# A changeover in a hybrid encoder layer: the order of sums, first products, forget gate and norm steps

## The chip, the cores and the metric

The kernel runs on one core of a Trainium2 chip. The metric is the device time of one execution in microseconds (us). Five engines share the work: PE (TensorE, matrix products), DVE (VectorE), ACT (ScalarE), POOL (GpSimd) and SP (SyncE, which only starts transfers here). Each engine runs its own instructions in order.

## The reference, cut to what matters

One layer of an encoder on 1024 tokens and 16 meta tokens put before them (L = 1040), width 1024, all in float32, followed by a mixture of experts.

```python
u = rms_norm(h, norm1_g)
p = u @ w_in                      # 1024 x 5384
a, bv, bg, q, k, v, fg, gates = split(p)
ya = pool_mixer(a) @ w_out_a
yb = silu(layer_norm(depthwise_conv(bv * sigmoid(bg)))) @ w_out_b
logf = log_sigmoid(fg + b_forget)                 # forget gate, 8 heads
yc = forgetting_attention(q, k, v, logf) @ w_out_c   # bias: cumsum of logf
g = sigmoid(gates.reshape(B, L, 3, D))
h = h + (g[:,:,0]*ya + g[:,:,1]*yb + g[:,:,2]*yc) @ w_o
h = h + hier_moe(rms_norm(h, norm2_g))            # 4 groups x 4 experts
out = rms_norm(h[:, 16:], final_g)
```

The change lies between the projection to v and the first attention scores: in the projections to q and to the gates (28 column tiles of 128), the forget gate and the convolution's layer norm.

## The kernel before, in words

Every float32 operand of a product is split into a high part (a cast on ACT, L172) and a low part (a subtraction on DVE, L173); a product is three passes, high by high, low by high and high by low. The transposed u lies in four slots: u4[0] and u4[1] hold the high parts of rows k 0 to 3 and 4 to 7, u4[2] and u4[3] the low parts (slot_94 to slot_97 in the rows below).

`run_jobs` runs jobs in the written order: k for four pairs of heads, then v (`v_all`, matmuls L586, evictions L172, L173 and L592, the last writing the forget gate's input `lf`), the job `forget`, and then `seven`. Long DVE work that has no due time stands in a list `pending`, from which `pump` takes some entries between products; `queue_sums` puts the sums of quarters of u there (L533 to L547, each 128 x 2048).

`seven` computes 14 pairs of column tiles (`PAIRS`: two of q, twelve of the gates). For each pair a product of a 2 x 2 block matrix by a 2 x 2 block of u is done with seven products instead of eight. The left operands are raw quarters of the weights and four POOL sums of them that `load` issues behind its DMA (left operands 1, 2 and 4 are raw quarters, 3, 5, 6 and 7 sums). The right operands are quarters of u (products 1, 2, 3), x (product 5, which is copied into u's place by L635 and L636) and the three sums tq[2], tq[3], tq[4] (products 6, 7, 4). A product is 12 matmuls of 128 x 512 (L678), so there are 98 products and 1176 such matmuls. Products of one pair add up in three PSUM banks: 1, 6, 5 and 3 in the first, 2 in the second, 7 and 4 in the third; pairs alternate between banks 0 to 2 and 5 to 7. After products 1, 6 and 5 ACT copies the bank's content of that moment into a buffer (`kept`, L683), and the next product of that bank adds on; after 2, 5 and 4 DVE adds the copy to a bank (`joined`, L687). `out_` scales and splits q and sends it to DRAM through POOL's queue (L697 to L701), or takes the sigmoid of a gate and sends it through SP's queue. The staging buffers are a ring of seven.

The table `order` sets the products' order; `parts` splits the left operand four products ahead. From product 11 on (counted from 0), one entry of the list `norm` is issued ahead of each product: the layer norm of the convolution in eight tiles of 128 tokens (`norm_steps`), each with five entries: `read` (a DMA), parts, `mean`, `root`, `result`. `mean` and `root` begin with two small matmuls by a matrix of ones (L484). `forget` is one piece: two activations with a table load each (L605, L606), two matmuls (L614, L615), eight small additions (L620), a transpose (L623) and a DMA.

`load(0)` and `load(1)` put their POOL sums over x and y (slot_1259).

Of the kernel before, what the change touches and what calls it, by code (L numbers as in the profile page):

```python
# [121 lines left out]
def body(tc, A, out):  # L122
# [3 lines left out]
    with es:  # L126
# [340 lines left out]
        def norm_steps(i, zs, hl):  # L467
            z, sq = zs[:, 0:2 * P], zs[:, 2 * P:4 * P]
            z2, sq2 = (x.rearrange("p (c t) -> p c t", c=2) for x in (z, sq))
            a, b = sq2[:, 0], sq2[:, 1]  # L470
            ts = slice(i * P, (i + 1) * P)
            o = {}

            def read():
                sy.dma_start(z2, dz.rearrange("p (c t) -> p c t", c=2)[:, :, ts])

            def parts(x):
                ve.tensor_add(a, x[:, 0], x[:, 1])
                split(a, *hl[1])

            def over_channels(n):
                o[n] = ps[:, 3 + n, 0:P]
                for part in range(2):
                    pe.matmul(o[n], ones, hl[1][part], start=part == 0, stop=part == 1)  # L484

            def mean():
                over_channels(0)
                ve.scalar_tensor_tensor(z2, o[0].unsqueeze(1).to_broadcast([P, 2, P]), -1.0 / 256, z2, ALU.mult, ALU.add)
                ac.activation(sq, z, AF.Square)
                parts(sq2)  # L490

            def root():

                over_channels(1)
                ve.tensor_scalar(a, o[1], 1.0 / 256, EPS, ALU.mult, ALU.add)
                ac.activation(b, a, AF.Ln)
                ac.activation(b, b, AF.Exp, scale=-0.5)
                ve.tensor_mul(a, a, b)
                ve.tensor_mul(a, a, b)
                ve.tensor_scalar(a, a, -0.5, 1.5, ALU.mult, ALU.add)  # L500
                ve.tensor_mul(b, b, a)

            def result():
                ve.tensor_mul(z2, z2, b.unsqueeze(1).to_broadcast([P, 2, P]))
                for ct in range(2):
                    ve.tensor_scalar(z2[:, ct], z2[:, ct], vec("conv_ln_g", ct), vec("conv_ln_b", ct), ALU.mult, ALU.add)
                ac.activation(sq, z, AF.Sigmoid)
                ve.tensor_mul(sq, z, sq)
                split(sq, hl[0][:, 0:2 * P], hl[0][:, 2 * P:4 * P])
                sy.dma_start(dy[1].rearrange("p (q t) -> p q t", q=4)[:, :, ts],  # L510
                             f32(hl[0]).rearrange("p (q t) -> p q t", q=4))
            return [read, lambda: parts(z2), mean, root, result]


        tq = {}
# [4 lines left out]
        def queue_sums():  # L520


            def begin():
# [3 lines left out]
                for n, x in zip((2, 4, 3), st["s_t"]):  # L527
                    tq[n] = [x.new([4, 512]) for _ in range(2)]

            def less(to, a, b):  # L530
                def first():
                    if b in st:
                        ve.tensor_sub(st[to], f32(uq(0, *a)), st[b])  # L533
                    else:
                        ve.tensor_sub(st[to], f32(uq(0, *a)), f32(uq(0, *b)))

                def low():
                    ve.tensor_add(st[to], st[to], f32(uq(1, *a)))

                def other():  # L540
                    ve.tensor_sub(st[to], st[to], f32(uq(1, *b)))
                return [first, low] + ([] if b in ("x", "y") else [other])

            def parts(n):
                def f():
# [4 lines left out]
                           less("y", (1, 0), "y") + parts(4) + less("y", (1, 1), (0, 1)) + parts(3))  # L550
# [48 lines left out]
        def forget(_):  # L599
# [13 lines left out]
            cum, tot = mm_bk.next()[:, 0:72], mm_bk.next()[:, 0:72]  # L613
# [8 lines left out]
            tp = mm_bk.next()[:72, 0:P]  # L622
# [3 lines left out]
            gp.dma_start(dF.rearrange("h (j c) -> (h j) c", c=P), fr[:72])  # L626
        job(lambda: None, forget)
# [4 lines left out]
        def seven():  # L632
            pump(1000)

            ac.copy(uq(0, 0, 1), st["x"])  # L635
            ve.tensor_sub(uq(1, 0, 1), st["x"], f32(uq(0, 0, 1)))  # L636
# [3 lines left out]
            st_sum = Ring([st["s_wx"].ap[:, n * 2048:n * 2048 + 2048] for n in range(2)])  # L640
# [3 lines left out]
            zs = small("sm512", 512).new([4 * P])  # L644
            norm = [f for i in range(8) for f in norm_steps(i, zs, hl)]
            left, tmp = {}, {}

            def load(n):
# [8 lines left out]
                gp.tensor_sub(s3, a[0, 0], a[1, 0])  # L657
                gp.tensor_add(s1, a[1, 0], a[1, 1])
                gp.tensor_sub(s2, s1, a[0, 0])
                gp.tensor_sub(s4, a[0, 1], s2)  # L660
# [47 lines left out]
            order = [(0, 1), (0, 2), (1, 1), (1, 2)]  # L708
            for n in range(len(PAIRS)):
                order += [(n, 7), (n, 6)] + ([(n, 2)] if n > 1 else []) + [(n, 5)]  # L710
# [4 lines left out]
            ahead = 0  # L715
            for at, (n, m) in enumerate(order):
                if (n, m) == (0, 4):
                    load(2)
                if m == 7 and 1 < n < len(PAIRS) - 1:
                    load(n + 1)  # L720
                while ahead < min(at + 5, len(order)):
                    parts(*order[ahead])
                    ahead += 1
                if at > 10 and norm:
# [12 lines left out]
                if n == len(PAIRS) - 1:  # L737
                    if m == 6:
                        st["s_t"][0].free(), st["s_t"][2].free()
# [5 lines left out]
            for x in (s_raw, s_hi, s_lo, st["s_wx"], st["s_t"][1], s_u[1], s_u[3], st["s_qk"]):  # L745
                x.free()
# [998 lines left out]
```

## Time and profile before

| what | value |
|---|---|
| median of 3 runs | 1193.0 us (1191.29 to 1194.4) |
| the profiled execution, its own time | 1193.69 us |
| its span in the trace | 1192.0 us |
| mean granted TensorE clock over the span | 0.951 |
| busy: PE, DVE, ACT, POOL | 1062.2, 823.1, 558.3, 400.9 us |
| matmuls L678 (products of halves) | 1176, 286.9 us busy |
| stretch from the first product matmul to the end of the norm's matmuls | 196.6 to 396.5 us |

How to read it: the span runs from the first to the last instruction in the trace, and the profiled execution's own time is 1.7 us longer. Busy times are of one engine each and lie beside each other. The granted clock is the share of TensorE's full speed (2.4 GHz) that was granted; 0.50 is its lower level (1.2 GHz). In a row with an idle time in brackets, the engine stood that long before the row's first instruction, and the releaser is the engine, tile and line that ended the wait.

### The profile page before, as it was taken

What the parts mean: (1) busy time and instruction counts of PE and PEld (TensorE: products, weight loads), DVE (VectorE), ACT (ScalarE), POOL (GpSimd) and SP (SyncE); (2) the same over time, 40 slices, a digit from 0 to 9 for tenths busy, and PEclk for the clock granted to TensorE, in tenths of its full rate; (3) what the DMA queues carried; (4) which work ended last, traced back from release to release, by engine and by line L of the source; (5) the groups of instructions that cost most, each with busy time, mean ns of one, the idle gap of its engine ahead of it and who ended that gap; (6) DMA issues with size and microseconds to landing.
All of it is one profiled execution on the core that took longest, in us unless ns stands there. A gap on an engine that the chain in (4) does not pass through costs nothing. (4 is left out here: it accounts for less than half of the span.)

```text
span 1192.0 us, 16417 instructions
## 1 busy us (share of the span) xinstructions
PE 1062.2 (89%) x5441; PEld 883.4 (74%) x5441; DVE 823.1 (69%) x1488; ACT 558.3 (47%) x1022; POOL 400.9 (34%) x463
## 2 busy tenths in 40 slices
PE   5999997899899999989999999899957989997972
PEld 5999996677677788867888888677745767775751
DVE  5799999665756534247888883577787764757864
ACT  5412223447676634367889520322234643535652
POOL 4001203452222422013333076200034654555654
PEclk9999998899999999989999999899977989999986
DMA  7412451253324332397892665333567896696973
GB/s 217 124 55 79 154 177 72 76 177 98 115 93 140 102 124 92 124 288 188 228 309 56 236 203 177 126 139 142 194 220 248 257 329 179 168 293 178 298 233 143
DMA packets 100552, 204.21 MB, mean 171 GB/s; under 512 B 11969, under 2 KB 57106, under 8 KB 99908
## 3 DMA queue, kind: packets, MB, share of 16 engines
q1 hardware_dynamic: 89204, 169.93, 44.8%
q0 software_dynamic: 10784, 31.13, 9.1%
q10 hardware_dynamic: 432, 1.57, 0.3%
q8 instruction: 60, 0.98, 0.3%
q14 instruction: 72, 0.59, 0.1%
HBM read 149.99 MB, written 59.35 MB: 176 GB/s over the span
## 5 line engine op out<-in xcount | busy, mean ns | idle before, releaser
L678 PE MATMUL ps<-slot,slot 128*128 128x512 f32 x1176 | 286.9, 403 | 11.4 <-DVE sm L592 7.8
L678 PEld LDWEIGHTS ps<-slot,slot 128*128 128x128 f32 x1176 | 224.5, 193 | 64.1 <-issue 8.2
L173 DVE TENSOR_TENSOR slot<-slot,slot 128x512 fp32r<-128x512 f32 (+3 forms) x228 | 228.1, 1021 | 56.4 <-ACT slot L172 51.1
L172 ACT CAST slot<-slot 128x512 fp32r<-128x512 f32 (+3 forms) x245 | 185.1, 786 | 172.9 <-PE ps L178 73.5
L178 PE MATMUL ps<-slot,slot 128*128 128x512 f32 (+3 forms) x1104 | 205.6, 347 | 0.9 <-ACT slot L252 0.9
L178 PEld LDWEIGHTS ps<-slot,slot 128*128 128x128 f32 x1104 | 186.9, 189 | 17.5 <-ACT slot L252 1.4
L1424 PE MATMUL ps<-slot,slot 128*128 128x512 f32 x552 | 143.0, 417 | 21.6 <-PEq L1706 13.0
L1424 PEld LDWEIGHTS ps<-slot,slot 128*128 128x128 f32 x552 | 109.5, 202 | 53.2 <-issue 19.2
L172 ACT CAST slot<-ps 128x512 fp32r<-128x512 f32 (+7 forms) x178 | 78.6, 463 | 77.7 <-PE ps L586 26.5
L1191 PE MATMUL ps<-slot,slot 128*128 128x512 f32 x384 | 100.2, 407 | 3.8 <-ACT slot L172 3.8
L178 PE MATMUL ps<-slot,sm 128*128 128x512 f32 x276 | 79.5, 438 | 23.0 <-DVE sm L1440 21.5
L173 DVE TENSOR_TENSOR slot<-ps,slot 128x512 fp32r<-128x512 f32 (+7 forms) x178 | 89.9, 532 | 8.4 <-ACT slot L172 7.5
L1191 PEld LDWEIGHTS ps<-slot,slot 128*128 128x128 f32 x384 | 70.5, 193 | 16.9 <-ACT slot L172 3.9
L178 PEld LDWEIGHTS ps<-slot,sm 128*128 128x128 f32 x276 | 54.7, 207 | 37.6 <-DVE sm L1440 24.1
L173 POOL TENSOR_TENSOR slot<-slot,slot 128x1024 fp32r<-128x1024 f32 x32 | 79.7, 2512 | 0.6 <-ACT slot L172 0.2
L456 DVE SCALAR_TENSOR_TENSOR slot<-slot,c,slot 128x1024 f32<-128x1024 f32 x60 | 74.9, 1283 | 0.5
L687 DVE TENSOR_TENSOR slot<-ps,slot 128x512 f32<-128x512 f32 x42 | 29.0, 690 | 58.0 <-PE ps L678 31.6
L657 POOL TENSOR_TENSOR slot<-slot 128x512 f32<-128x512 f32 x14 | 20.2, 1445 | 144.3 <-DMA slot<-in_w_in_dram 138.9
L819 DVE CUSTOM_DVE_ANT_0 slot<-ps,slot 128x656 f32<-128x656 f32 (+7 forms) x64 | 49.3, 771 | 24.1 <-PE ps L814 17.2
L949 POOL TENSOR_TENSOR slot<-slot,slot 128x512 f32<-128x512 f32 x32 | 47.3, 1501 | 38.3 <-DVE slot L948 34.2
L874 PE MATMUL ps<-const,slot 128*128 128x128 f32 x352 | 58.9, 278 | 1.5 <-DVE slot L173 1.2
L183 POOL TENSOR_SCALAR stats<-stats 128x1 f32<-128x1 f32 (+1 forms) x24 | 16.0, 667 | 118.9 <-ACT slot L182 118.3
(285 smaller groups left out, 1572.7 us busy)
## 6 DMA issues: line engine op xcount, KB each, us to landing
slot<-in_exp_w_dram SPq DMA_DIRECT2D x96, 512.0 KB, 6.6
slot<-in_w_in_dram SPq DMA_DIRECT2D x14, 1024.0 KB
dg<-slot SPq DMA_DIRECT2D x48, 256.0 KB, 2.0
slot<-dk SPq DMA_DIRECT2D x32, 260.0 KB, 8.4
slot<-in_x_dram SPq DMA_DIRECT2D x16, 512.0 KB, 3.4
slot<-dg SPq DMA_DIRECT2D x16, 512.0 KB, 6.2
slot<-in_w_in_dram SPq DMA_DIRECT2D x10, 512.0 KB, 7.0
slot<-dF SPq DMA_DIRECT2D x8, 520.0 KB
```

The source lines that it names most:

```text
L172: ac.copy(hi, raw)
L173: (lo_eng or ve).tensor_sub(lo, raw, f32(hi))
L178: pe.matmul(o, a, b, start=i == 0, stop=i == len(ops) - 1)
L456: ve.scalar_tensor_tensor(acc[:, ct, :], src, wk, acc[:, ct, :], ALU.mult, ALU.add)
L657: gp.tensor_sub(s3, a[0, 0], a[1, 0])
L678: pe.matmul(o, x[:, k, :], y[:, k, :], start=i == 0 and m in (1, 2, 7), stop=i == 11 and m in (2, 3, 4), skip_group_check=True)
L687: ve.tensor_add(t, bank(n, m), t)
L819: ve.tensor_tensor_reduce(out=s2, in0=o, in1=n2, scale=-1.0, scalar=3.0e38, op0=ALU.add, op1=ALU.min, accum_out=mn)
L874: pe.transpose(tp[:, t * P:(t + 1) * P], p_of(g, i0 + t)[:, b * P:(b + 1) * P], ident)
L949: gp.tensor_add(m, m, t)
L1191: pe.matmul(o[:, c, :], a, b, start=n == 0, stop=n == 23)
L1424: pe.matmul(o, x[:, k, :], wk, start=q == 0 and i == 0, stop=q == 1 and i == len(ops) - 1)
```

## The change

- **Sums.** The order is now tq[2], tq[3], tq[4]. The last one (`last_sum`: four DVE operations, of which L535 is one more than before, the cast L545 and the subtraction L546) is no longer in `pending`; it is issued in `seven` behind the splits of the first four left operands.
- **Copies and POOL.** The copy of x (now L719, L720) is issued behind the first two splits, POOL's sums for the first pair behind it, and those for the second pair behind the last sum.
- **Order.** The first pair's products 6 and 7 come before its 5; `load(2)` is issued one product earlier.
- **Forget gate.** `forget` is a generator in three steps, issued ahead of products 6, 9 and 12 (counted from 0), on banks 3 and 4; its result goes out through SP's queue.
- **Norm.** It begins ahead of product 14 and has four empty entries per tile, so that a product more lies between two steps.

```diff
@@ norm_steps
-            return [read, lambda: parts(z2), mean, root, result]
+            rest = lambda: None
+            return [read, rest, lambda: parts(z2), rest, mean, rest, root, rest, result]
-        tq = {}
+        tq, last_sum = {}, []
@@ queue_sums
-                for n, x in zip((2, 4, 3), st["s_t"]):
+                for n, x in zip((2, 3, 4), st["s_t"]):
...
+                if a == to:
+                    ops.append(lambda: ve.tensor_sub(st[to], st[to], f32(uq(0, *b))))
+                else:
+                    ops.append(lambda: ve.tensor_sub(st[to], f32(uq(0, *a)), st[b] if b in st else f32(uq(0, *b))))
+                    ops.append(lambda: ve.tensor_add(st[to], st[to], f32(uq(1, *a))))
+                if b not in ("x", "y"):
+                    ops.append(lambda: ve.tensor_sub(st[to], st[to], f32(uq(1, *b))))
...
             pending.extend([begin] + less("x", (0, 1), (0, 0)) + less("y", (1, 1), "x") + parts(2) +
-                           less("y", (1, 0), "y") + parts(4) + less("y", (1, 1), (0, 1)) + parts(3))
+                           less("y", "y", (0, 0)) + parts(3))
+            last_sum.extend(less("y", (1, 0), "y") + less("y", "y", (0, 0)) + parts(4))
@@ forget
+            yield
-            cum, tot = mm_bk.next()[:, 0:72], mm_bk.next()[:, 0:72]
+            cum, tot = ps[:, 3, 0:72], ps[:, 4, 0:72]
             pe.matmul(cum, tri, x_, start=True, stop=True)
...
+            yield
-            tp = mm_bk.next()[:72, 0:P]
+            tp = ps[:72, 3, P:2 * P]
...
-            gp.dma_start(dF.rearrange("h (j c) -> (h j) c", c=P), fr[:72])
-        job(lambda: None, forget)
+            sy.dma_start(dF.rearrange("h (j c) -> (h j) c", c=P), fr[:72])
@@ seven
             pump(1000)
-
-            ac.copy(uq(0, 0, 1), st["x"])
-            ve.tensor_sub(uq(1, 0, 1), st["x"], f32(uq(0, 0, 1)))
...
-            st_sum = Ring([st["s_wx"].ap[:, n * 2048:n * 2048 + 2048] for n in range(2)])
+            st_sum = Ring([st["s_wx"].ap[:, n * 2048:n * 2048 + 2048] for n in (1, 0)])
...
-                gp.tensor_sub(s3, a[0, 0], a[1, 0])
-                gp.tensor_add(s1, a[1, 0], a[1, 1])
-                gp.tensor_sub(s2, s1, a[0, 0])
-                gp.tensor_sub(s4, a[0, 1], s2)
+                def sums():
+                    gp.tensor_add(s1, a[1, 0], a[1, 1])
+                    gp.tensor_sub(s2, s1, a[0, 0])
+                    gp.tensor_sub(s3, a[0, 0], a[1, 0])
+                    gp.tensor_sub(s4, a[0, 1], s2)
+                if n > 1:
+                    sums()
+                else:
+                    first.append(sums)
...
-            order = [(0, 1), (0, 2), (1, 1), (1, 2)]
+            order = [(0, 1), (0, 2), (1, 1), (1, 2), (0, 6), (0, 7)]
...
             load(0), load(1)
-            ahead = 0
+            for n in range(2):
+                parts(*order[n])
+
+            ac.copy(uq(0, 0, 1), st["x"])
+            ve.tensor_sub(uq(1, 0, 1), st["x"], f32(uq(0, 0, 1)))
+            first[0]()
+            for n in range(2, 4):
+                parts(*order[n])
+            for f in last_sum:
+                f()
+            first[1]()
+            ahead = 4
+            gate = forget()
             for at, (n, m) in enumerate(order):
-                if (n, m) == (0, 4):
+                if (n, m) == (0, 3):
                     load(2)
...
+                if at in (6, 9, 12):
+                    next(gate, None)
...
-                if at > 10 and norm:
+                if at == 14:
+                    zs = small("sm512", 512).new([4 * P])
+                    norm = [f for i in range(8) for f in norm_steps(i, zs, hl)]
+                if at >= 14 and norm:
                     norm.pop(0)()
```

The lines behind L547 move by a few: L678 is L679 after the change, L683 is L684, L687 is L688, L697 is L698.

DVE at the end of the projection to v, before (sm_20 holds the last 16 rows of v, sm_21 the forget gate, slot_1259 x and y, slot_1262 the last sum, slot_91 to slot_93 raw weights and their high and low parts):

```order
L636 TENSOR_TENSOR slot_96<-slot_1259,slot_94 128x4x512
L173 TENSOR_TENSOR slot_750<-ps,slot_750 128x3x64
L592 TENSOR_TENSOR sm_21_1198<-ps,c_2_76 128x8
L547 TENSOR_TENSOR slot_1262<-slot_1259,slot_1262 128x2048
L173 TENSOR_TENSOR sm_20_1196<-ps,sm_20_1196 16x4
L173 TENSOR_TENSOR sm_20_1196<-ps,sm_20_1196 16x60
L173 TENSOR_TENSOR slot_93<-slot_91,slot_92 128x512
L173 TENSOR_TENSOR sm_20_1196<-ps,sm_20_1196 16x3x64
L592 TENSOR_TENSOR sm_21_1198<-ps,c_2_76 16x8
```

and now:

```order
L538 TENSOR_TENSOR slot_1259<-slot_1259,slot_97 128x2048
L173 TENSOR_TENSOR slot_750<-ps,slot_750 128x3x64
L592 TENSOR_TENSOR sm_21_1198<-ps,c_2_76 128x8
L173 TENSOR_TENSOR sm_20_1196<-ps,sm_20_1196 16x4x64
L173 TENSOR_TENSOR slot_93<-slot_91,slot_92 128x512 x3
L173 TENSOR_TENSOR sm_20_1196<-ps,sm_20_1196 16x4
L173 TENSOR_TENSOR sm_20_1196<-ps,sm_20_1196 16x60
L173 TENSOR_TENSOR slot_93<-slot_91,slot_92 128x512
L173 TENSOR_TENSOR sm_20_1196<-ps,sm_20_1196 16x3x64
L592 TENSOR_TENSOR sm_21_1198<-ps,c_2_76 16x8
L720 TENSOR_TENSOR slot_96<-slot_1259,slot_94 128x4x512
L535 TENSOR_TENSOR slot_1259<-slot_1259,slot_94 128x2048
```

The four splits of left operands and v's last eviction (L592, 16x8) now stand ahead of x's low part and of the last sum, and no operation of 128x2048 stands between v's last evictions.

ACT around the forget gate's table loads, before (slot_750 is the ring of staging buffers):

```order
L172 CAST sm_20_1196<-ps 16x3x64
L172 CAST slot_92<-slot_1259 128x512 x2
L605 ACT_TABLE_LOAD
L605 ACTIVATE sm_21_1198<-sm_21_1198 128x72
L172 CAST slot_92<-slot_1259 128x512
L606 ACT_TABLE_LOAD
L606 ACTIVATE sm_21_1198<-sm_21_1198 128x72
L172 CAST slot_92<-slot_1259 128x512 x2
L683 COPY slot_750<-ps 128x512
```

and now:

```order
L684 COPY slot_750<-ps 128x512
L545 CAST slot_1262<-slot_1259 128x2048
L698 ACTIVATE slot_750<-slot_750 128x512
L684 COPY slot_750<-ps 128x512
L172 CAST slot_92<-slot_1259 128x512 x2
L698 ACTIVATE slot_750<-slot_750 128x512
L172 CAST slot_92<-slot_1259 128x512 x2
L605 ACT_TABLE_LOAD
L605 ACTIVATE sm_21_1198<-sm_21_1198 128x72
L684 COPY slot_750<-ps 128x512
L606 ACT_TABLE_LOAD
L606 ACTIVATE sm_21_1198<-sm_21_1198 128x72
```

The table loads stood ahead of any copy of a bank; now kept copies (L684) stand ahead of the first, and one between it and the second.

PE between `mean` and `root` of the second norm tile, before (slot_1262 is a sum of u, lists the parts of the norm's operand):

```order
L678 MATMUL ps<-slot_97,slot_92 128x512 x4
L484 MATMUL ps<-lists_1766,ones_85 128x128 x2
L678 MATMUL ps<-slot_94,slot_92 128x512 x4
L678 MATMUL ps<-slot_94,slot_93 128x512 x4
L678 MATMUL ps<-slot_96,slot_92 128x512 x4
L484 MATMUL ps<-lists_1766,ones_85 128x128 x2
```

and now:

```order
L679 MATMUL ps<-slot_96,slot_92 128x512 x4
L484 MATMUL ps<-lists_1737,ones_85 128x128 x2
L679 MATMUL ps<-slot_95,slot_92 128x512 x4
L679 MATMUL ps<-slot_95,slot_93 128x512 x4
L679 MATMUL ps<-slot_97,slot_92 128x512 x4
L679 MATMUL ps<-slot_1262,slot_92 128x512 x4
L679 MATMUL ps<-slot_1262,slot_93 128x512 x4
L679 MATMUL ps<-slot_1262,slot_92 128x512 x4
L484 MATMUL ps<-lists_1737,ones_85 128x128 x2
```

Twelve product matmuls stood between the two pairs of norm matmuls; now there are 24.

## Rows read from the trace of the kernel before

**Rows 1.** Page, header: the span
```profile
span 1192.0 us, 16417 instructions
```

**Rows 2.** PE timeline: start, us, engine, line, op, tiles, shape, xcount [idle before <-releaser]
```profile
196.59 1.09 PE L678 MATMUL ps<-slot,slot 128*128 128x512 f32 x4
205.44 0.76 PE L678 MATMUL ps<-slot,slot 128*128 128x512 f32 x1 [7.77 <-DVE sm L592]
...
216.25 0.67 PE L614 MATMUL ps<-sm,c 128*128 128x72 f32 x2 [4.73 <-DVE sm L618]
...
217.10 4.53 PE L678 MATMUL ps<-slot,slot 128*128 128x512 f32 x11
...
221.49 30.00 PE L678 MATMUL ps<-slot,slot 128*128 128x512 f32 x128
```

**Rows 3.** Windows: start:end, length, busy (x) of PE, PEld, DVE, ACT, POOL, PEclk, DMA share, GB/s
```profile
245.90:396.50 150.60, 137.16 (x571) 107.18 (x569) 90.64 (x175) 98.66 (x167) 44.61 (x36) 0.97 0.35 116
218.00:220.00 2.00, 2.00 (x6) 1.52 (x6) 1.08 (x6) 0.00 (x0) 0.00 (x0) 0.50 0.00 0
...
326.00:330.00 4.00, 4.00 (x13) 3.28 (x12) 1.49 (x5) 2.86 (x5) 0.00 (x0) 0.59 0.00 0
```

**Rows 4.** Waits of PE, 245.9 to 396.5: us in total, times, longest
```profile
PE ps L484 <- ACT lists L172: 6.0, 7, 2.0
PE ps L484 <- DVE lists L173: 4.9, 4, 1.2
PE ps L678 <- ACT slot L683: 2.5, 1, 2.5
```

**Rows 5.** PE timeline, one norm tile's matmuls and the products behind them
```profile
369.54 0.33 PE L484 MATMUL ps<-lists,ones 128*128 128x128 f32 x1 [0.37 <-ACT lists L172]
371.08 0.33 PE L484 MATMUL ps<-lists,ones 128*128 128x128 f32 x1 [1.21 <-DVE lists L173]
...
374.29 17.10 PE L678 MATMUL ps<-slot,slot 128*128 128x512 f32 x73
```

**Rows 6.** DVE timeline, around the changeover
```profile
197.44 2.29 DVE L636 TENSOR_TENSOR slot<-slot,slot 128x2048 fp32r<-128x2048 f32 x1
...
199.99 3.29 DVE L547 TENSOR_TENSOR slot<-slot,slot 128x2048 fp32r<-128x2048 f32 x1
...
207.78 7.41 DVE L173 TENSOR_TENSOR slot<-slot,slot 128x512 fp32r<-128x512 f32 x5
...
221.98 0.68 DVE L173 TENSOR_TENSOR slot<-slot,slot 128x512 fp32r<-128x512 f32 x1
```

**Rows 7.** POOL timeline, two of the eight sums at the changeover
```profile
199.88 1.26 POOL L657 TENSOR_TENSOR slot<-slot 128x512 f32<-128x512 f32 x1 [5.47 <-DVE slot L636]
...
201.67 2.73 POOL L658 TENSOR_TENSOR slot<-slot 128x512 f32<-128x512 f32 x1
```

**Rows 8.** ACT timeline, around the changeover
```profile
195.37 1.91 ACT L635 CAST slot<-slot 128x2048 fp32r<-128x2048 f32 x1
...
220.47 0.59 ACT L683 COPY slot<-ps 128x512 f32<-128x512 f32 x1 [4.84 <-PE ps L678]
220.95 0.62 ACT L172 CAST slot<-slot 128x512 fp32r<-128x512 f32 x1
```

**Rows 9.** ACT groups, 245.9 to 396.5: xcount | busy us, mean ns | idle before
```profile
L497 ACT ACT_TABLE_LOAD x7 | 9.0, 1283 | 0.1
...
L497 ACT ACTIVATE sm<-sm 128x128 f32<-128x128 f32 x7 | 2.2, 313 | 0.1
```

**Rows 10.** SP, ACT and POOL timelines: a load, its use, a DMA to dq, the copy behind it
```profile
227.20 12.89 SPq L652 DMA_DIRECT2D slot<-in_w_in_dram  x2
...
234.39 1.15 ACT L172 CAST slot<-slot 128x512 fp32r<-128x512 f32 x2 [1.79 <-DMA slot<-in_w_in_dram]
...
250.73 0.54 POOL L701 DMA_DIRECT2D dq<-slot  x1
...
253.48 0.59 ACT L683 COPY slot<-ps 128x512 f32<-128x512 f32 x1 [6.43 <-DMA dq<-slot]
```

More of the change, by code (lines that the diff above doesn't have):

```diff
@@ L526, in begin @@
                 st["s_t"] = [sl.take(F32R) for _ in range(3)]
-                for n, x in zip((2, 4, 3), st["s_t"]):
+                for n, x in zip((2, 3, 4), st["s_t"]):
                     tq[n] = [x.new([4, 512]) for _ in range(2)]
             def less(to, a, b):
[L531 to L542, printed above, removed]
+                ops = []
+                if a == to:
[5 more added lines that the diff above has]
+                    ops.append(lambda: ve.tensor_sub(st[to], st[to], f32(uq(1, *b))))
+                return ops
             def parts(n):
@@ L597, in body, with forget @@
         job(lambda: [win_unit(COL_V + half * 260, 260, k0, k0 + 4) for half in range(2) for k0 in (0, 4)], v_all, 1)
-        def forget(_):
+        def forget():
             x_, t, u = (st["s_f"].new([72]) for _ in range(3))
@@ L643, in seven, with load @@
             t_r, hl = Ring(qk_r.b[0:7]), (qk_r.b[7], small("lists", 2 * P + 120, F32R).ring(P, 2).b)
[L644 to L648, printed above, removed]
+            left, tmp, first = {}, {}, []
+            def load(n, sums=True):
                 b, i = PAIRS[n]
@@ L705, in out_ @@
                 sy.dma_start(dg[b, i + d, :, cs], t)
-            order = [(0, 1), (0, 2), (1, 1), (1, 2)]
+            order = [(0, 1), (0, 2), (1, 1), (1, 2), (0, 6), (0, 7)]
             for n in range(len(PAIRS)):
-                order += [(n, 7), (n, 6)] + ([(n, 2)] if n > 1 else []) + [(n, 5)]
+                order += ([(n, 7)] if n else []) + ([(n, 6)] if n else []) + ([(n, 2)] if n > 1 else []) + [(n, 5)]
                 if 0 < n < len(PAIRS) - 1:
@@ L738, in seven @@
                     if m == 6:
-                        st["s_t"][0].free(), st["s_t"][2].free()
+                        st["s_t"][0].free(), st["s_t"][1].free()
                         attention_start()
@@ L744, in seven @@
                         first_scores()
-            for x in (s_raw, s_hi, s_lo, st["s_wx"], st["s_t"][1], s_u[1], s_u[3], st["s_qk"]):
+            for x in (s_raw, s_hi, s_lo, st["s_wx"], st["s_t"][2], s_u[1], s_u[3], st["s_qk"]):
                 x.free()
```

## Prediction

> **What bounds the kernel now.** I read the header, then PE's timeline, its clock, its waits, and last the timelines of DVE, ACT and POOL around the stops. The span is 1192.0 us [rows 1]; the profiled execution took 1193.69 us, 1.7 more, and lies 0.7 above the median of 1193.0. The sum is made against 1193.7. The stages behind the products keep their instruction order on every engine, so what is gained or lost before 396.5 us shifts them.
>
> In the stretch of the change PE is the bound, and it loses time in two places. The first is the changeover from v to the products [rows 2]: PE does four product matmuls at 196.59, stands 7.77 us for DVE's last eviction of v, later 4.73 us for the forget gate's additions, and has done 4 + 1 + 12 + 11 = 28 product matmuls by 221.49. Behind each stop it is slow: after the second, 11 matmuls take 4.53 us where eleven cost 2.6, and the granted clock at 218 to 220 is 0.50, the lower of its two levels [rows 2, 3]. One 128x512 matmul at full rate is 17.10/73 = 0.234 us [rows 5]. The second place is the norm between the products [rows 4, 5]: a norm matmul waits for ACT's or DVE's part, 0.37 and 1.21 us in the tile shown. From 245.9 to 396.5 these waits come to 6.0 + 4.9, with 2.5 for one kept copy: 13.4 us. In the same stretch the clock averages 0.97, so 0.03 x 150.6 = 4.5 us are lost at the lower level, as at 326 to 330, where PE is busy throughout at 0.59 [rows 3]. As a check: 538 product matmuls by 0.234 are 125.9, 32 norm matmuls some 2.7, together 128.6; the stretch is 150.6, 22.0 more, of which these terms explain 17.9.
>
> **Term A, the changeover.** I compare the moment X at which 132 product matmuls (11 products) and the gate's three are done. Before: 221.49 + 104 x 0.234 = 245.9. After, step by step:
>
> 1. v's last eviction on DVE ended at 205.4, where PE went on [rows 2]. It no longer stands behind x's low part (2.29 us) and a sum that took 3.29 [rows 6]: 205.4 - 2.3 - 3.3 = 199.8, and 199.4 with POOL not yet slowing the low part ahead of it (step 2). The product that needs its bank is now the third, which PE reaches at 196.6 + 24 x 0.234 = 202.2. The 7.77 us go. I leave 0.4 for the first operand's cast: four products end at 197.0 + 48 x 0.234 = 208.2.
> 2. What is late next is the left operand of product 6, a sum on POOL. POOL starts when x's low part has been read, 199.4 + 2.3 = 201.7, and its third sum ends 3 x 1.26 later [rows 7], at 205.5; the cast is 0.62 [rows 8]. Its low part stands on DVE behind two long sums and another low part (2.3 + 0.7 + 2.3 + 0.7, 207.7). With none of these slowed PE does not wait. But a long DVE sum beside POOL took 3.29 instead of 2.29, five low parts 1.48 each instead of 0.68, and a POOL sum 2.73 instead of 1.26 [rows 6, 7]. All slowed: 211.3, where PE needs it at 209.1. So 0 to 2.2 us.
> 3. A new stop. The second pair's POOL sums overwrite y and wait for the last sum, whose low part ends at 213.1 (slowed: 215.7). Four sums and a DMA issue make 5.7 (7.4) us. On ACT, the last of their casts, the gate's first table load with its activation (1.28 + 0.31) [rows 9], and only then the kept copy of product 5 (0.59) follow: 221.5 (225.9). PE has done 36 + 4 more matmuls and stands there at 217.5 (219.7): a stop of 4.0 to 6.2, priced in X.
> 4. The other 44 matmuls take 10.3, the gate's three 0.5, and slow matmuls behind the stop cost 2.0, as after the stop of 4.73 (4.53 - 11 x 0.234). X is 234.3 to 238.7.
>
> One DVE operation more (L535) and the gate's DMA on SP instead of POOL lie beside this; the extra 2.3 us of DVE are in step 2. The gate's additions now have three products (8.4 us) between steps; I cost them at nothing, 4.73 if that cover were missing. I take the middle of both ends, since DVE and POOL overlap for part of these steps only: X = 236.5, **gain A 9.4 us** (7.2 to 11.6; without any stop in step 3, X would be 228.4 and the gain 17.5).
>
> How a slowed DVE sum comes about matters here: the sum of 2.29 took 3.29 exactly while POOL was summing [rows 6, 7]. The Trainium skill, "SBUF — State Buffer", section "SBUF: two separate sides", says that DVE and GpSimd share a port pair as an exclusive lock, held for the whole instruction, so that the other blocks fully. By that rule, which speaks against this change, the sum would be that of rival 2, 1172.7 us instead of 1168.0. The rows agree that both are slowed, but a strict alternation would make a low part and a sum 0.68 + 1.26 = 1.94 together, where the five low parts came 1.48 apart [rows 6, 7], so it is a rival and not the forecast.
>
> **Term B, the norm.** A step's parts were followed by 4 to 12 product matmuls (0.9 to 2.8 us) before the norm matmul that reads them; now by 24 or more (5.6 us), but for the first `root`. A norm wait on top of this cover was at most 2.0 [rows 4], so it vanishes. I keep one pair, 0.37 + 1.21 = 1.6 [rows 5], for the root that still has twelve. With the waits the lower clock should go too, since it fell behind waits. The 2.5 of the kept copy goes if its buffer is free in time (rival 1). **Gain B 13.4 + 4.5 - 1.6 = 16.3 us.** Its bounds: half of it, 8.2, if the clock and the longer waits stay, and 20.4 if the other 4.1 of the 22.0 go too.
>
> The two table loads fewer on ACT in this stretch are not on the path. **Sum: 1193.7 - 9.4 - 16.3 = 1168.0 us.**
>
> **Rivals.**
>
> 1. *A second stop for a buffer.* The kept copy of the second pair's product 5 needs a staging buffer that a transfer of q still reads. That transfer is issued on POOL behind two sums of `load(3)`. A load took 234.39 - 227.20 = 7.2 us to be used, a transfer to dq 253.48 - 250.73 = 2.7 [rows 10]. `load(3)` can be issued some 3 us behind the copy of step 3, at 224.5 to 228.9; 7.2, two sums (2.6), two issues (1.1) and 2.7 later the copy can start: 238.1 to 242.5, done at 239 to 243. PE needs it at X + 24 x 0.234 = 239.9 to 244.3. If it is missed as before: 2.5 + 1.5 for the clock, 1172.0 us. For: the margin is 1 us. Against: both move with step 3.
> 2. *Strict alternation of DVE and POOL.* Then step 2's low part ends near 212.8, the last sum near 217.2, and the second pair's four sums with four DVE operations between (4 x 1.26 + 4 x 0.69 + 0.55 = 8.4) at 225.6; the copy is done at 228.4, X = 241.2, gain A 4.7: 1172.7 us. For: every row of a DVE operation beside POOL is longer. Against: the low parts above.
> 3. *Only half of the norm's loss goes*, because parts queue behind other work of ACT: 1168.0 + 8.1 = 1176.1 us. For: ACT is also where 6.0 of the waits end [rows 4]. Against: its longest wait was 2.0.
> 4. *Slower: kept copies behind the norm's table loads.* `root` puts two table loads and activations on ACT, and a gate's sigmoid between them a third. A kept copy behind all of them comes 3 x 1.28 + 2 x 0.31 + 0.60 + 0.59 = 5.65 us late; with the next product of its bank 2.8 us away, PE stands 2.85 and loses some 1.6 more to the clock, 4.4 per tile. In eight tiles this is 35.6: 1203.6 us. It decides from (25.7 + 3.6)/8 = 3.7 us per tile on. For: in the new order a kept copy stands directly behind the second load in most tiles. Against: the same loads ran seven times each before [rows 9], and PE waited once for a kept copy, for a transfer's sake [rows 4, 10].
>
> That the change doesn't do what it says can be excluded by the order of instructions: 24 matmuls stand where 12 stood.
>
> **How the numbers follow.** Forecast as summed 0.68, rival 1 0.13, rival 2 0.10, rival 3 0.04, rival 4 0.03, and 0.02 for two losses that leave no change. The range reaches from A without half of the new stop and B at its upper bound (1168.0 - 4.0 - 4.0 = 1160) to rival 3 with a part of rival 1 on top, 1180. A measurement of this kernel can tell about 0.3%, 3.6 us, from no change. Faster by more than that: 0.95, within 0.02, slower 0.03.
>
> **What would show it.** In the profile after: no wait of the product matmuls for L592 and none of the gate's matmuls for the additions; instead one wait of PE for L684 on ACT, 4 to 6 us, between 217 and 226. Waits of L484 of at most some 2 us in total, and a clock near 1.00 in the norm's stretch. The 132nd product matmul at 236.5, the last of the 1176 some 26 us earlier, the later stages only shifted. It would be wrong if L484's waits stay above 5 us, if L684 stops PE in every norm tile, or if the later stages give time back.

## The result and the profile after

The changed kernel takes 1173.7 us (median of 4 runs, 1172.23 to 1177.8), the kernel before beside it 1193.7 us (1191.29 to 1198.58): the ratio is 0.984 with an interval from 0.9803 to 0.9877, some 19 us. The forecast was 1168.0 us, the range 1160 to 1180. The profiled execution took 1177.8 us, the longest of the four; its span is 1176.1 us, 15.9 below that of [rows 1].

One mark divides the gain: the first attention score's matmul, behind all but a few of the products. Before, and then after, on PE's timeline:

```profile
513.06 0.41 PE L813 MATMUL ps<-slot 128*128 128x264 f32 x2
```

```profile
495.43 0.41 PE L831 MATMUL ps<-slot 128*128 128x264 f32 x2
```

17.6 us are gained there; behind it this execution gives 1.7 us back. The stretch behind the mark, which no edit here touches, takes 673.9 to 682.2 us in this case's 14 traces; 1.7 us lie well within that, and the mark tells the parts of the change apart better than the whole time does. PE's timeline after, from the first product on; these rows answer to [rows 2] and [rows 5]:

```profile
195.76 12.39 PE L679 MATMUL ps<-slot,slot 128*128 128x512 f32 x52
210.76 7.68 PE L679 MATMUL ps<-slot,slot 128*128 128x512 f32 x32 [2.61 <-DVE slot L173]
218.88 1.20 PE L679 MATMUL ps<-slot,slot 128*128 128x512 f32 x4 [0.43 <-ACT slot L172]
223.97 8.46 PE L679 MATMUL ps<-slot,slot 128*128 128x512 f32 x24 [3.88 <-ACT slot L684]
...
232.63 4.89 PE L679 MATMUL ps<-slot,slot 128*128 128x512 f32 x20
241.98 0.43 PE L625 MATMUL ps<-const,sm 128*72 128x128 f32 x1 [4.46 <-DVE sm L622]
242.06 21.88 PE L679 MATMUL ps<-slot,slot 128*128 128x512 f32 x84
...
311.63 7.40 PE L679 MATMUL ps<-slot,slot 128*128 128x512 f32 x24 [2.29 <-ACT slot L684]
...
388.51 8.64 PE L679 MATMUL ps<-slot,slot 128*128 128x512 f32 x36 [1.45 <-ACT slot L684]
```

The wait of 7.77 us for v's last eviction is gone. Four stops of 2.61, 0.43, 3.88 and 4.46 us stand in the changeover instead, and 132 product matmuls with the gate's three are done at 242.06 us, where it was 245.9: 3.9 us gained. The other 13.7 of the 17.6 come from the norm's stretch: no matmul of L484 waits any more, where [rows 4] had 10.9 us, and two kept copies stop PE there for 3.7. The clock in the windows, with the columns of [rows 3]:

```profile
220.00:230.00 10.00, 6.12 (x16) 4.74 (x16) 6.73 (x13) 6.31 (x11) 5.54 (x8) 0.66 0.54 183
240.00:250.00 10.00, 8.02 (x26) 6.41 (x27) 4.08 (x10) 1.74 (x3) 2.22 (x2) 0.66 0.12 38
260.00:300.00 40.00, 40.00 (x179) 32.58 (x178) 20.67 (x39) 26.07 (x45) 11.01 (x8) 1.00 0.40 131
```

It is lower behind the two longest stops and at full speed from 260 to 300, in the norm's stretch. How the stop of 4.46 us comes about is on DVE's timeline after, between the gate's matmuls (232.3) and its transpose:

```profile
233.00 2.08 DVE L173 TENSOR_TENSOR slot<-slot,slot 128x512 fp32r<-128x512 f32 x1 [2.19 <-ACT slot L172]
235.01 0.68 DVE L688 TENSOR_TENSOR slot<-ps,slot 128x512 f32<-128x512 f32 x1
235.61 0.16 DVE L621 TENSOR_TENSOR sm<-sm,ps 128x8 f32<-128x8 f32 x1
235.68 1.11 DVE L173 TENSOR_TENSOR slot<-slot,slot 128x512 fp32r<-128x512 f32 x1
236.71 1.77 DVE L699 SCALAR_TENSOR_TENSOR slot<-slot 128x512 fp32r<-128x512 f32 x1
238.41 0.77 DVE L621 TENSOR_TENSOR sm<-sm,ps 128x8 f32<-128x8 f32 x4
239.09 2.09 DVE L173 TENSOR_TENSOR slot<-slot,slot 128x512 fp32r<-128x512 f32 x1
241.10 0.56 DVE L621 TENSOR_TENSOR sm<-sm,ps 128x8 f32<-128x8 f32 x3
```

The eight additions (L621) need 1.5 us, but between them stand low parts and q's scaling, each 1.1 to 2.1 us long where 0.68 is the undisturbed value [rows 6]; POOL makes four sums of later pairs between 234.60 and 242.3. So DVE is done with the additions and the subtraction behind them at 241.93, 9.1 us after the gate's matmuls (232.83). The third step is written three products behind the second, but a step's place in the written order is not its place on PE: only 20 matmuls, 4.89 us, stand there between the gate's matmuls and its transpose.

The stop of 3.88 us, on ACT's timeline: the last cast of the second pair's POOL sums, the gate's first table load, and only then the kept copy for which PE stands.

```profile
221.25 0.62 ACT L172 CAST slot<-slot 128x512 fp32r<-128x512 f32 x1 [1.18 <-POOL slot L657]
221.88 1.28 ACT L605 ACT_TABLE_LOAD   x1
223.18 0.26 ACT L605 ACTIVATE sm<-sm 128x72 f32<-128x72 f32 x1
223.35 0.57 ACT L684 COPY slot<-ps 128x512 f32<-128x512 f32 x1
```

And the stop of 2.29 us in the norm: the same kind of copy stands on ACT behind the cast of the next norm tile's part, which waits for DVE, which waits for the tile's read.

```profile
310.80 0.30 ACT L172 CAST lists<-sm 128x128 fp32r<-128x128 f32 x1 [1.48 <-DVE sm L478]
311.00 0.58 ACT L684 COPY slot<-ps 128x512 f32<-128x512 f32 x1
```

### The profile page after: what moved, and what is told of

Same layout as the page of the kernel before. It is cut to its first block, busy times and chain, and to the rows that moved or that the text cites. A ratio compares the mean times of both kernels' runs of the same rounds, so it can differ in the third digit from the quotient of the medians.

```text
span 1176.1 us, 16394 instructions
## 1 busy us (share of the span) xinstructions
PE 1058.0 (90%) x5441; PEld 883.2 (75%) x5441; DVE 824.1 (70%) x1489; ACT 554.1 (47%) x1020; POOL 400.0 (34%) x462
## 5 line engine op out<-in xcount | busy, mean ns | idle before, releaser
L679 PE MATMUL ps<-slot,slot 128*128 128x512 f32 x1176 | 285.3, 402 | 11.6 <-ACT slot L684 8.6
L679 PEld LDWEIGHTS ps<-slot,slot 128*128 128x128 f32 x1176 | 223.6, 192 | 65.6 <-ACT slot L684 10.8
L1442 PEld LDWEIGHTS ps<-slot,slot 128*128 128x128 f32 x552 | 109.1, 201 | 52.9 <-issue 19.7
L172 ACT CAST slot<-ps 128x512 fp32r<-128x512 f32 (+7 forms) x178 | 78.8, 463 | 79.8 <-PE ps L586 25.7
L183 POOL TENSOR_SCALAR stats<-stats 128x1 f32<-128x1 f32 (+1 forms) x24 | 16.3, 679 | 118.0 <-ACT slot L182 117.4
L839 ACT ACTIVATE slot<-slot,sm 128x656 f32<-128x656 f32 (+7 forms) x64 | 50.9, 795 | 7.0 <-DVE sm L837 6.7
```

The costliest lines, as they stand in the source:

```text
L172: ac.copy(hi, raw)
L679: pe.matmul(o, x[:, k, :], y[:, k, :], start=i == 0 and m in (1, 2, 7), stop=i == 11 and m in (2, 3, 4), skip_group_check=True)
L839: return lambda: ac.activation(s[:, 0:w], s[:, 0:w], AF.Exp, bias=mn, scale=-1.0, accum_out=sm[:, 8 + i:9 + i])
L1442: pe.matmul(o, x[:, k, :], wk, start=q == 0 and i == 0, stop=q == 1 and i == len(ops) - 1)
```

## Experiments

All ratios are to the kernel before, run on the same chip beside them.

### The parts apart

**The rests alone**: the kernel before with the list of nine entries (its product line is L679 here, v's eviction L593).

```diff
-            return [read, lambda: parts(z2), mean, root, result]
+            rest = lambda: None
+            return [read, rest, lambda: parts(z2), rest, mean, rest, root, rest, result]
```

> The kernel before with the empty norm entries alone. Theory (the gain is the sum of a norm part and a changeover part): the 10.9 us of waits of the norm's matmuls go and most of the 4.5 us at the lower clock, the changeover keeps its stops of 7.8 and 4.7 us; 1193.7 - 9 to 14 = about 1182 us. Rival (the changeover gave nothing on balance, the rests are the whole change): about 1174 us.

Measured: 1178.9 us, ratio 0.9878 (0.9855 to 0.9901). PE's waits from 190 to 500 us:

```profile
PE ps L679 <- DVE sm L593: 7.8, 1, 7.8
PE ps L679 <- ACT slot L684: 6.3, 5, 2.5
PE ps L615 <- DVE sm L619: 4.7, 1, 4.7
```

The changeover's stops are as before, the norm's waits are gone, and the first score comes at 498.76, 14.3 us earlier. The rests carry most of the gain.

**The changeover alone**: the changed kernel with the five entries.

```diff
-            return [read, rest, lambda: parts(z2), rest, mean, rest, root, rest, result]
+            return [read, lambda: parts(z2), mean, root, result]
```

> The changed kernel with the norm's list of five entries as before. Theory: only the changeover's 4 to 8 us are gained, about 1187 us, with 8 to 11 us of waits of the norm's matmuls back. Rival (rests are the whole change): about 1193 us.

Measured: 1193.2 us, ratio 0.9984 (0.9962 to 1.0006): nothing. PE has its 132 matmuls at 242.5, 3.4 us earlier, but reaches the first score at 514.76, 1.7 us later. The rival's number came, not its reason: the gain was there and was lost in the norm. DVE's waits there, 246 to 400 us, say where from:

```profile
DVE sm L478 <- DMA sm<-dz: 8.5, 5, 4.1
```

Before, this wait was 2.4 us in total. The read of a norm tile (L475) is issued on SP's queue, and here one is issued at 310.02, 3.6 us behind a load of weights (306.47).

**The same, the norm from product 18**:

```diff
-                if at == 14:
+                if at == 18:
...
-                if at >= 14 and norm:
+                if at >= 18 and norm:
```

> The changed kernel without the empty norm entries (as e2_no_rests), the norm beginning ahead of product 18 instead of 14. A pair has seven products, and 18 is 11 + 7: the norm's steps meet the pair's steps as in the kernel before, which began at 11. Theory (without rests the changeover's gain was lost because the read of the norm's tile was issued behind a load of weights and came 3 to 4 us late): DVE's waits for that read fall from 8.5 to some 2.5 us, PE's waits of the norm's matmuls from 14 to 11, and the time is 4 to 7 us below e2_no_rests, at about 1187 us, ratio 0.993 to the kernel before. Rival (the time depends on how far the changeover runs ahead, not on the meeting of steps): as e2_no_rests, ratio 0.998.

Measured: 1190.3 us, ratio 0.997 (0.9945 to 0.9996). DVE's wait for the read and PE's waits for the norm's parts:

```profile
DVE sm L478 <- DMA sm<-dz: 2.0, 2, 1.1
```

```profile
PE ps L484 <- ACT lists L172: 7.6, 7, 3.1
...
PE ps L484 <- DVE lists L173: 3.6, 3, 1.2
```

The waits fall as the theory said, from 8.5 to 2.0 and from 14.2 to 11.2 us, and the first score comes 3.3 us earlier. In time the two differ by 1.7 us (by the ratios) and their intervals overlap; the 1187 us of the theory did not come. So the traces speak for the phase between the norm's steps and the seven products of a pair as one cause of the lost gain, the times do not settle it, and whether it is the whole is open.

### The new stops

**The gate's third step later**, on the changed kernel:

```diff
-                if at in (6, 9, 12):
+                if at in (6, 9, 17):
...
-                if at == 14:
+                if at == 19:
```

(and the norm's condition `at >= 19`).

> The changed kernel with the forget gate's third step (the transpose) ahead of product 17 instead of 12 and the norm's start moved from 14 to 19. Theory: PE's wait of 4.5 us for the gate's additions and some 2.2 us of slow matmuls behind it go, nothing takes their place: about 1173.7 - 6.7 = 1167 us. Rival (PE would have stood at the same place for something else, a kept copy whose buffer a transfer of q still reads, or the operands behind POOL's sums): 1172 to 1174 us, with a wait of 3 us or more for another releaser between 235 and 245 us.

Measured: 1169.7 us, ratio 0.9789 (0.9762 to 0.9815). PE runs through where it stood 4.46 us:

```profile
238.16 16.00 PE L679 MATMUL ps<-slot,slot 128*128 128x512 f32 x68 [0.26 <-ACT slot L684]
```

With 24 matmuls ahead of these, 92 now stand between the gate's matmuls and its transpose (254.00). The stop was a real loss, and nothing of its size took its place. The theory's 6.7 us fit: the first score comes at 489.9, 5.6 us earlier, although PE stood there 1.46 us for a load of k.

**All three steps later**: `at in (14, 18, 22)`, the norm from 24.

> The changed kernel with all three steps of the forget gate later (ahead of products 14, 18 and 22, norm from 24), the products' order as in the change. Theory: the stop of 4.5 us with 2.2 of slow matmuls goes as with the third step alone, and the stop of 3.9 us shrinks by the table load and its activation, to some 2.3: 7 to 9 us less than the changed kernel beside it. Rival (the loss comes back elsewhere, as a kept copy's or a buffer's wait): 4 us less or fewer.

Measured: 1166.5 us, ratio 0.9789 (0.9773 to 0.9805), 11 us less than the changed kernel run beside it (1177.9) and 8.4 us earlier at the first score than in its trace (486.40 for 494.80). The stop for the kept copy is 2.31 us instead of 3.07 there and 3.88 in the first profile. A new one appears, of 1.34 us at 240.5: ACT's copy waits 5.14 us for a transfer to dq.

**Steps later, and product 4 ahead of product 3 in the first pair**:

```diff
-                order += [(n, 3), (n, 4)]
+                order += [(n, 3), (n, 4)] if n else [(n, 4), (n, 3)]
```

> The changed kernel with the forget gate's steps ahead of products 14, 18 and 22 (norm from 24) and the first pair's product 4 ahead of its product 3. Theory: the table load no longer stands ahead of the kept copy of product 5, and 2.8 us more lie between that copy and the product that adds on; the stop of 3.9 us at 220 and some 2.8 us of slow matmuls behind it go as well: about 1173.7 - 6.7 - 6 = 1161 us. Rival (buffer or transfer waits take their place): 1167 us or more.

Measured: 1169.3 us, ratio 0.9804 (0.9781 to 0.9828). A miss:

```profile
231.05 31.32 PE L679 MATMUL ps<-slot,slot 128*128 128x512 f32 x125 [5.94 <-DVE slot L688]
```

Product 4 adds on to product 7's bank, which DVE has to read first, together with the kept copy of product 5: the wait for the copy came back as a longer one.

**Steps later, and the kept copy of product 5 ahead of the second pair's casts on ACT** (ACT's written order held from product 5 to 9, the splits of two products held back):

```diff
+                if at == 5:
+                    held = ExitStack()
+                    held.enter_context(tc.manual_schedule(engines={ET.Activation}))
+                if at == 10:
+                    held.close()
-                while ahead < min(at + 5, len(order)):
+                while at not in (5, 6) and ahead < min(at + 5, len(order)):
```

> As the kernel with all three gate steps later, and besides ACT's order held by hand between products 5 and 9: the splits of the second pair's sums are issued behind the kept copy of product 5. Theory (those casts hold up the copy because they wait for POOL's sums, which wait for the last sum): the stop ahead of product 3 falls below 1 us, and with its slow matmuls another 3 to 4 us go: 10 to 13 us less than the changed kernel. Rival (the operands then come too late themselves): a wait of 2 us or more for L172 or L173 some products later and 9 us less or fewer.

Measured: 1172.2 us, ratio 0.983 (0.9807 to 0.9853). The copy's stop is gone, as intended, but the scheduler now put the gate's matmuls right behind it:

```profile
223.09 0.41 PE L615 MATMUL ps<-sm,c 128*128 128x72 f32 x2 [4.39 <-DVE sm L612]
...
240.78 31.32 PE L679 MATMUL ps<-slot,slot 128*128 128x512 f32 x128 [3.42 <-ACT slot L684]
```

The rival held, by another wait than it named. Whether the copy's place is worth something by itself is not told by this run.

### The last sum's place

**The changed kernel again**, run beside three of the others (all three steps later, the kept copy first, and the last sum back in the list).

> The changed kernel, unaltered, beside the three others of this call, so that they are compared with it on one chip. Expected at 1173 to 1176 us with the stops that its first profile showed (2.6, 0.4, 3.9, 4.5 us before 245 us).

Measured: 1177.9 us, ratio 0.9876 (0.9854 to 0.9898). Its stops are 2.59, 3.07 and, for the additions, 5.51 us. This is the ratio of the rests alone (0.9878): what the changeover adds to them, 3.3 to 4.0 us at the first score, is not told apart from nothing in these times.

**The last sum back in the list of long DVE work**, all else as changed:

```diff
+                           less("y", "y", (0, 0)) + parts(3) +
+                           less("y", (1, 0), "y") + less("y", "y", (0, 0)) + parts(4))
-            last_sum.extend(less("y", (1, 0), "y") + less("y", "y", (0, 0)) + parts(4))
```

> The changed kernel with the last sum back in the list of long DVE work, so that it is issued ahead of the first operands as before; all else as changed. Theory (moving the sum is what lets the first four products start at once): v's last eviction stands behind two long DVE operations and a subtraction again, PE stops 5 to 8 us at its first products, but POOL's second sums come earlier and the stops of 2.6 and 3.9 us go: about as long as the changed kernel, -1 to +4 us. Rival (the sum's place decides little, the waits of v's eviction don't return): 3 us or more faster than the changed kernel.

Measured: 1167.9 us, ratio 0.9797 (0.9779 to 0.9815): 10 us less than the changed kernel beside it, of which its trace shows 3.8 at the first score (491.01 for 494.80). The theory fell. PE, and on DVE the first two low parts and v's last eviction:

```profile
197.14 3.08 PE L679 MATMUL ps<-slot,slot 128*128 128x512 f32 x12
200.57 4.91 PE L679 MATMUL ps<-slot,slot 128*128 128x512 f32 x20 [0.35 <-DVE slot L173]
210.18 15.63 PE L679 MATMUL ps<-slot,slot 128*128 128x512 f32 x56 [4.70 <-ACT slot L172]
...
229.23 11.47 PE L679 MATMUL ps<-slot,slot 128*128 128x512 f32 x42 [2.50 <-ACT slot L684]
```

```profile
199.84 1.27 DVE L173 TENSOR_TENSOR slot<-slot,slot 128x512 fp32r<-128x512 f32 x2
...
203.58 0.15 DVE L592 TENSOR_TENSOR sm<-ps,c 16x8 f32<-16x8 f32 x1
```

That eviction is only 1.6 us earlier than before (205.14), and PE does not wait for it: 28 matmuls stand ahead of the product that needs its bank. In the kernel before, one matmul of that product stood fifth on PE, and everything behind it waited. The matmuls next in line would have waited there too, for a low part that came 1.2 us later [rows 2, 206.68]; here the copy of x stands behind the first two splits, and their low parts are done at 201.1. So the 7.77 us go with the order of PE and of the first low parts, and the last sum's place is not needed for it. The stop of 4.46 us is gone with the gate's steps where the change has them, but not because DVE is faster: the additions take 8.3 us from the gate's matmuls on (226.21 to 234.48) where they took 9.1. On PE the gate's matmuls stand behind 88 product matmuls instead of 112, and 44 instead of 20 stand between them and the transpose; why the order comes out so is not shown. A stop of 2.50 us for a kept copy remains.

**Both: the last sum first and the gate later**, the two edits above together.

> The last sum back in the list of long DVE work (as e7_sum_first) and the forget gate's steps ahead of products 14, 18 and 22 (as e4_gate_later). Theory (both cure the same loss, POOL's second sums and the gate meeting before 245 us): the gains of 10 and 11 us over the changed kernel don't add up; 1164 to 1168 us, ratio 0.976 to 0.980 to the kernel before. Rival (independent causes): some 20 us less than the changed kernel, ratio 0.970 to 0.972.

Measured: 1176.3 us, ratio 0.9853 (0.9813 to 0.9894). A miss for both. ACT's and PE's rows:

```profile
249.93 0.58 ACT L684 COPY slot<-ps 128x512 f32<-128x512 f32 x1 [8.79 <-DMA dq<-slot]
```

```profile
250.57 16.67 PE L679 MATMUL ps<-slot,slot 128*128 128x512 f32 x60 [4.98 <-ACT slot L684]
```

This is the forecast's first rival, in full: the copy's staging buffer is still read by a transfer of q that stands on POOL behind sums of `load(3)`, and that load could be used only at 242.9.

**The first pair's POOL sums over y, ahead of the copy of x; those of the second pair over x, behind it** (with the last sum first, and the gate later):

```diff
-            st_sum = Ring([st["s_wx"].ap[:, n * 2048:n * 2048 + 2048] for n in (1, 0)])
+            st_sum = Ring([st["s_wx"].ap[:, n * 2048:n * 2048 + 2048] for n in (0, 1)])
...
             load(0), load(1)
+            first[0]()
...
-            first[0]()
+            first[1]()
             for n in range(2, 4):
                 parts(*order[n])
-            for f in last_sum:
-                f()
-            first[1]()
```

> As e12_sum_first_gate_later, with POOL's sums for the first pair over y, which is free when the last sum's low part is made, and those of the second pair over x, behind its copy. Theory: the first operand that needs POOL comes earlier by the copy of x, some 2 us; but DVE's operations of 2.3 us hold POOL's first sum up as in e7_sum_first (4.80 us instead of 1.26), so that 0 to 3 us are gained against e12: 1162 to 1167 us. Rival (the order of POOL's sums decides the stop of 4.7 us at 205): 5 us or more gained.

Measured: 1168.3 us, ratio 0.9777 (0.974 to 0.9814). The stop of 4.7 us at 205 stays, so the order of POOL's sums does not decide it; the transfer's wait is down to 0.46 us, and that for the kept copy ahead of it from 2.62 to 0.71. That is 8 us less than the run before, not 0 to 3: the size of the rival, without its mechanism.

**The same with the gate as in the change** (6, 9, 12, norm from 14):

> As e11_sums_early_gate_later, but with the forget gate's steps ahead of products 6, 9 and 12 and the norm from 14 as in the change. Theory (POOL's sums of the first two pairs being made early is what lets DVE make the gate's additions in time, as e7_sum_first showed): no wait of 2 us or more of the gate's matmuls for DVE, ratio 0.976 to 0.981 to the kernel before, 10 us or so below the changed kernel. Rival (the gate's place is needed as well): a wait for the additions of 3 us or more comes back, ratio 0.984 or more.

Measured: 1167.2 us, ratio 0.9772 (0.9744 to 0.9800), below both intervals of the changed kernel (from 0.9803 and from 0.9854 on). The gate's waits come to 0.73 us, and all 132 matmuls are done at 236.3:

```profile
224.93 0.41 PE L615 MATMUL ps<-sm,c 128*128 128x72 f32 x2 [0.73 <-DVE sm L619]
...
236.32 0.27 PE L625 MATMUL ps<-const,sm 128*72 128x128 f32 x1
```

The forecast held, its reason is not shown: the additions take 9.6 us here (225.57 to 235.13), and the stop is gone because 47 matmuls stand ahead of the transpose. This version beats both kernels, and keeps the written places of the gate, the rests and the products' order of the change; it gives up the late last sum and moves POOL's sums.

## Why the prediction was right, and where it failed

**Term A failed in the sentence behind step 4, on the gate's additions**: "I cost them at nothing, 4.73 if that cover were missing". It measured 4.46 us (5.51 in the repeat). X came at 242.06 instead of 236.5, and gain A was 3.9 instead of 9.4. The cover was miscounted on both engines. "Three products (8.4 us)" is the written distance; on PE 20 matmuls stood there, 4.7 us at 0.234. And I did not count what stood on DVE between the additions, which made 1.5 us of work last 9.1. With three products in place the stop would have been some 0.7 us (an estimate, 9.1 - 8.4), so the larger part is the count on PE. The price was in the text, on the wrong side. The run with the third step alone moved shows it: 92 matmuls, no stop, although the additions took 10.4 us (232.28 to 242.73). So do the two runs with 44 and 47.

The other steps of A: step 1's wait went as said, and its bank's product did stand third; but the run with the last sum first shows that moving the sum was not needed for it. Step 2's 0 to 2.2 us measured 2.61; 0.43 more went to an operand of the second pair. Step 3's stop is where it was put, behind that cast and that table load: 3.88 for 4.0 to 6.2, done at 223.9 for 221.5 to 225.9. The 2.0 us of slow matmuls behind it were 2.8 (24 took 8.46, at full rate 5.6).

**Term B was right in its mechanism, 2.6 us too large**: 13.7 for 16.3. All waits of L484 went, not all but 1.6, and the clock is 1.00 from 260 to 300. Some 2.2 us of the shortfall are slow matmuls behind the gate's stop, which fall into this stretch: 84 took 21.88 where another 84 of the norm took 19.7. What I left out is that a longer cover for PE does nothing for ACT's queue: a kept copy stands behind a norm cast that waits for DVE, 2.29 and 1.45 us (in the first of them DVE waits for a read), and slow matmuls behind the first. That is a milder form of rival 4's head of the queue, without its table loads. The sum of the two terms, 25.7, measured 17.6 at the first score.

**The rivals.** Rival 1 did not come in the changed kernel. It came in two of the runs without the stop of 4.46 us, 1.34 and 4.98 us, but not in the run with the third step alone moved, so it is not that stop alone that gives its transfer time. Rival 2's time, 1172.7, is nearest to the median, but not by its mechanism: the copy was done at 223.9, not at 228.4, and the rest of X is the gate. Yet the argument against it misread a row: the five low parts that "came 1.48 apart" are four in 6.81 us, each beside a POOL sum, and one of 0.68 after the last of these sums. Before, on DVE and then POOL:

```profile
207.78 6.81 DVE L173 TENSOR_TENSOR slot<-slot,slot 128x512 fp32r<-128x512 f32 x4
```

```profile
210.65 1.72 POOL L659 TENSOR_TENSOR slot<-slot,slot 128x512 f32<-128x512 f32 x1
```

Each of the four ends some 0.55 us after a sum has ended, and each sum behind the first 1.13 us after a low part: they do take turns, one pair in 1.70 us. That is less than 0.68 + 1.26 because part of each one's time, some 0.13 us (an estimate from these rows), passes while it waits. Rival 3's half of B did not stay. Rival 4 did not come. The range held because it took in losses of this size; that A's shortfall was of another kind is luck. Of the signs named ahead, the one on the gate's additions failed; those on L484 and on L592 came, and that on L684 nearly (3.88 us for 4 to 6, with two shorter ones in the norm).

**What the change's parts are worth.** The rests some 14 us, the changeover 3 to 4 at the first score with them and nothing without them; the late last sum in it costs about 4 there and 5 to 10 in time (0.9797 against 0.984 and 0.9876).

## What to carry to other kernels

Cover is to be counted in the order in which the engine runs, and against all that stands on the engine that makes the awaited value: three written products were 20 matmuls on PE, and eight additions of 1.5 us took 9.1 on DVE, with low parts between them. Where one engine stops for another in order, look also at which instruction stands in front on the waiting engine (a single matmul held back all behind it) before speeding up the engine it waits for. And after taking one stop away look for a transfer that is now waited for: the same edit, the gate later, was worth 11 us in the changed kernel (8.4 at the first score) and cost some 7 (by the ratios, 0.9797 and 0.9853; 6.4 at the first score) with the last sum first.

## What the runs showed of the hardware

A POOL sum and a long DVE operation do not share, they wait for each other. After, on DVE and then on POOL:

```profile
200.31 2.27 DVE L535 TENSOR_TENSOR slot<-slot,slot 128x2048 f32<-128x2048 f32 x1
...
206.72 3.38 DVE L540 TENSOR_TENSOR slot<-slot,slot 128x2048 f32<-128x2048 f32 x1
```

```profile
200.52 3.22 POOL L654 TENSOR_TENSOR slot<-slot 128x512 f32<-128x512 f32 x1 [6.08 <-DVE slot L720]
...
206.33 1.63 POOL L657 TENSOR_TENSOR slot<-slot,slot 128x512 f32<-128x512 f32 x1
```

POOL's first sum starts beside L535, which ends at 202.58, and ends 1.16 us after it, about its time alone (1.26) [rows 7]; L540 starts beside L657 and ends 2.14 us after POOL did, about its time alone. With the last sum first, POOL's first sum is held for a whole run of DVE operations:

```profile
203.46 4.80 POOL L654 TENSOR_TENSOR slot<-slot 128x512 f32<-128x512 f32 x1 [3.24 <-DVE slot L546]
```

```profile
203.65 2.27 DVE L720 TENSOR_TENSOR slot<-slot,slot 128x2048 fp32r<-128x2048 f32 x1
205.85 1.27 DVE L173 TENSOR_TENSOR slot<-slot,slot 128x512 fp32r<-128x512 f32 x2
207.06 0.67 DVE L688 TENSOR_TENSOR slot<-ps,slot 128x512 f32<-128x512 f32 x1
```

It ends at 208.26, 1.14 us after the last operation with two operands in SBUF and 0.53 after one that has only one there. The Trainium skill, "SBUF — State Buffer", section "SBUF: two separate sides", calls the shared port pair an exclusive lock that a DVE operation with two SBUF inputs takes against a GpSimd operation that reads SBUF. By these rows the trace agrees, and the forecast weighed the rule too lightly. What I had not expected is that POOL's first sum here gets no turn between three DVE operations that follow each other without a gap; between the low parts of the kernel before it got one each time (1.70 us apart, above). What decides this is open.

In these two executions the clock is not settled by a stop's length. At the same place the changed kernel stood 2.29 us and 24 matmuls took 7.40 us behind it [the timeline after], with a granted clock of 0.77 from 311.6 to 319.1; in the repeat it stood 2.51 us, and they took 5.83 at 1.00 (312.5 to 318.5):

```profile
312.59 5.83 PE L679 MATMUL ps<-slot,slot 128*128 128x512 f32 x24 [2.51 <-ACT slot L684]
```

So 1.6 us behind one stop differ between two executions of one program, which may be part of why single times spread by 5 us.
